# One column pair of the MLP as eight products, feature sums inside the head, modulation moved between layers

## The chip, the cores and the metric

The kernel runs on one core of a Trainium2 chip. The metric is device time in microseconds (us) of one execution; the time before is the median of 3 runs. One more execution was recorded by the hardware profiler, and all rows below come from it. The engines are named as in the profile: PE (matmul), PEld (weight load, beside PE), DVE (vector), ACT (scalar activations), POOL (GpSimd), SP (the queue that issues the loads).

## The reference

Two layers of a hybrid backbone are computed for 640 tokens: 512 sample tokens on a grid and 128 context tokens, model width 1024. Cut to what matters here, each layer is

```python
shift1, scale1, gate1, shift2, scale2, gate2 = silu(cond) @ w_mod + b_mod   # 6 x 1024
h = rms_norm(x, norm1_g) * (1 + scale1) + shift1
z = h @ w_in                      # pooling, q, k, v, LRU, gates
...
h_seq, h_final = rg_lru(conv_centred(u_lru), ...)     # scans over the tokens
merged = g0 * (pool_o @ w_branch[0]) + g1 * (attn_o @ w_branch[1]) + g2 * (lru_o @ w_branch[2])
x = x + gate1 * (merged @ w_out)
h2 = rms_norm(x, norm2_g) * (1 + scale2) + shift2
x = x + gate2 * (square(relu(h2 @ w_up)) @ w_down)    # w_up 1024 x 4096
```

All arrays are float32. The second layer's modulation (the first line) needs only the conditioning vectors, so the kernel may compute it at any time before its use.

## The kernel before, in words

**Tokens and precision.** Activations lie transposed: 128 features on the partitions, 640 tokens in two halves of 320 (`HALF`). Every operand is split into a high and a low part, and one product is three matmuls per 128 rows of weights (high x high, high x low, low x high; `product`, lines 248 to 259). So one column block of 128 output features for one half takes 8 x 3 = 24 matmuls of 128x320 in the mixers and in the first four column blocks of the MLP, and 12 where the depth is 512. Weights come by DMA into three `raw` buffers and are split by ACT (high part, line 227) and DVE (low part, line 228).

**The list of work.** `build_layer` appends items in the order in which PE is to work; the loop at the end of `hybrid_step_kernel` walks the list and issues loads and splits ahead. After each product `tick` runs one step of two queues of generators (`side_a`, `side_b`) and closures that were deferred by a number of ticks. A scheduler then orders the instructions of each engine; every engine works in that order.

**The MLP.** The 4096 columns of `w_up` are 8 blocks `b` of 512, each two pairs `e` of 256 columns. Block 0 is the **head**: a group of four items, each with 2 x 24 matmuls. It starts while the second half of `h2` is not yet made: `head` first does the first 12 matmuls of each item on the first half (`head_low`), calls `second()` (`norm_second`: statistics matmul `nps`, line 446, then DVE, ACT and POOL), and then the rest. The head's products are read out of PSUM by `evict_up` (DVE line 1190, ACT lines 1191 and 1192, DVE line 1193). The other 14 pairs are items of kind `st`: `st_body` computes a pair of column blocks over both halves by **seven** products of 12 matmuls (lines 295 to 297) in place of eight, from sums of weight blocks (POOL, lines 272 to 275, in `st_begin`) and sums of feature blocks (`T1` to `T4`). These feature sums are made once per layer by the generator `sums` (POOL lines 1236, 1239, 1246, 1256; DVE 1237, 1240, 1242, 1257, 1259; split by ACT 1227 and DVE 1228), in two parts `c` of 640 columns each and then `T4`. It is put on `side_b` when the head is over, runs a step per tick of the down products, and what is left is run (`drain`) ahead of the first `st` item:

```python
        down(0, 0, 2)
        up(1, 0)
        down(0, 4)
        up(1, 1)
        down(0, 6)
        for b in range(2, 8):
            up(b, 0)
            down(b - 1, 0, 2)
            up(b, 1)
            down(b - 1, 4, 6)
```

`down(b, m)` multiplies block `b`'s 512 squared features by two column blocks of `w_down` (four products of 12 matmuls), and DVE adds them to `x` (`x_update`, line 498).

**Modulation.** 12 chunks of 512 outputs per layer; a chunk is four items of kind `modv` (256 rows of `w_mod`), each of them four DVE instructions of 128x512 (lines 517 and 519), with a summing matmul (`mps`, line 525) and transposes (`mcol`, line 506) on PE per chunk. `mod_next()` puts the next such item behind the item just added. In layer 0's MLP, items of 6 chunks of the second layer are put behind every `up` and `down` until they are used up; the other 6 chunks are spread in the second layer's mixers. The first layer has 8 chunks in its own mixers, at the same places of the code.

**LRU.** The generator `lru` on `side_b` makes, for each of four channel blocks, the convolution, its split `xs` (ACT line 953, DVE 954), then after `LY` ticks the gate matmuls `lps` (line 964), activations, scans and the product with the gelu branch; `split_act` splits the result into `lh` for the third branch's products (`mm<-lh`).

Of the kernel before, what the change touches and what calls it, by code (L numbers as in the profile page):

```python
# [36 lines left out]
PY = 2  # L37
LY = 1
SY = 0
# [17 lines left out]
def hybrid_step_kernel(  # L57
# [285 lines left out]
    def head(its, done, evict, second=None):  # L343

        h = state["h"]
        for e, it in enumerate(its):
            head_low(it["i"])
            if e == 1 and second:
                second()
        for e, it in enumerate(its):  # L350
            evict(e, 0, product(it, 0, 0, h, 8, range(4, 8), it["ps"]))
            tick()
        for e, it in enumerate(its):
            evict(e, 1, product(it, 0, 1, h, 8))
            tick()
            done()
# [694 lines left out]
    def build_layer(l):  # L1051
# [130 lines left out]
        if l + 1 < DEPTH:  # L1182
            mod_todo.extend((l + 1, n, kk) for n in range(6) for kk in range(4))

# [10 lines left out]
        def up_body(b, e):  # L1195
# [13 lines left out]
            def body(it):  # L1209
                if (b, e) == (1, 0):  # L1210
                    drain(side_b)
# [4 lines left out]
                if (b, e) == (7, 1):  # L1216
                    del L["T"]
            return body

        def sums():  # L1220
# [13 lines left out]
            for c in range(2):  # L1234
# [14 lines left out]
                yield  # L1249
            state["h"] = None  # L1250
            out["T4"] = unit("T4", [128, 2, 4, HALF])
            b12 = None
            for c in range(2):
# [60 lines left out]
        def up(b, e):  # L1314
            add("st", up_pair(b, e), up_body(b, e), more_bias if (l, b, e) == (0, 2, 0) else
                late_h if (l, b, e) == (1, 2, 0) else None)
            items[-1]["i"] = len(items) - 1
            mod_next()

        def down(b, *ms):  # L1320
            for m in ms:
                add("k4", down_src(b, m), down_body(b, m))
                mod_next()

        def up_head(its, done):
            head(its, done, lambda *a: evict_up(0, *a), lambda: norm_second(l, 1))
            side_b.append(("sums", sums()))

        add_group("k8", [up_src(i) for i in range(4)], up_head, pre_up)
        down(0, 0, 2)  # L1330
        up(1, 0)
        down(0, 4)
        up(1, 1)
        down(0, 6)
        for b in range(2, 8):
# [4 lines left out]
        if l + 1 < DEPTH:  # L1340
            add_group("k4", [down_src(7, m) for m in range(0, 8, 2)], down_tail)
            mod_todo.extend((l + 1, n, kk) for n in range(6, 12) for kk in range(4))
        else:
# [237 lines left out]
```

## Time and profile before

| what | value |
|---|---|
| median of 3 runs | 2170.62 us (2170.19 to 2172.32) |
| the profiled execution | 2169.2 us, its span 2167.4 us |
| mean granted clock of PE | 0.99 of full speed |
| PE busy | 2104.7 us, 97% of the span |
| DVE, ACT, POOL busy | 70%, 47%, 25% of the span |
| HBM | 204.76 MB read, 101 GB/s over the span |

The span is the time from the first to the last instruction; the execution's own time is 1.8 us longer. PE's matmuls overlap: the 311 ns of a row is the length of one, not the distance between two, so PE's pace is read from counts of matmuls per stretch.

### The profile page before, as it was taken

Reading aid. Unit: us, or ns where it says so; the run is one execution under the profiler, and the core shown is the slowest. Engines: PE = TensorE matmul, PEld = TensorE weight load, DVE = VectorE, ACT = ScalarE, POOL = GpSimd, SP = SyncE. Lnnn points to the kernel's source line nnn. Section 1 sums busy time; section 2 is a strip of 40 time slices with the busy share of each in tenths; the row PEclk is TensorE's granted clock in tenths of the full one; section 3 lists DMA queues with packets and bytes.
Section 4 is the critical chain, followed back from the end, with each engine's and each line's share of the span. In section 5 each row is a group of like instructions: output and inputs, shape, how many; then the busy total and the mean of one; then the engine's idle time right before and its main releaser. Section 6 shows DMA issues by size and latency. Waiting matters only on the chain.

```text
span 2167.4 us, 35837 instructions
## 1 busy us (share of the span) xinstructions
PE 2104.7 (97%) x13892; PEld 1989.1 (92%) x13892; DVE 1507.1 (70%) x2937; ACT 1019.3 (47%) x2068; POOL 542.1 (25%) x575
## 2 busy tenths in 40 slices
PE   8999999999998899999999999999999989999999
PEld 3988899999998889899999888999999979999999
DVE  4777766667768988876677775675854777666665
ACT  4765427673244433333356654277633544333332
POOL 2444301242204221231024441012421232111110
PEclk9999999999999999999999999999999999999999
DMA  9322243324532344432341122432243212222222
GB/s 323 102 62 81 77 138 99 96 81 151 175 98 68 98 121 133 126 98 79 98 136 50 56 68 75 146 104 77 79 126 124 72 49 79 78 79 78 80 87 78
DMA packets 246914, 218.16 MB, mean 101 GB/s; under 512 B 11077, under 2 KB 214361, under 8 KB 246745
## 3 DMA queue, kind: packets, MB, share of 16 engines
q1 hardware_dynamic: 246744, 215.88, 32.7%
q8 instruction: 109, 1.79, 0.3%
q14 instruction: 61, 0.49, 0.1%
HBM read 204.76 MB, written 13.12 MB: 101 GB/s over the span
## 4 chain that ended last, share of the span: by engine, by line
PE 75%; DVE 12%; DMA 4%; ACT 4%; POOL 3%; issue 2%; SPq 0%; POOLq 0%; ACTq 0%; DVEq 0%
PE mm L256 18%; PE mm L258 17%; PE mm L257 17%; PE mm L295 3%; PE mm L297 3%; PE mm L296 3%; DVE macc L519 2%; PE o L772 2%; DVE wlo L228 1%; DMA raw<-in_w_mod_dram 1%; DVE t L465 1%; PE mmz L295 1%; PE mmz L297 1%; PE mmz L296 1%; PE ptt L759 1%
## 5 line engine op out<-in xcount | busy, mean ns | idle before, releaser
L256 PE MATMUL mm<-h,whi 128*128 128x320 f32 x1536 | 486.9, 317 | 6.0 <-DVE rl L1190 2.9
L257 PE MATMUL mm<-h,whi 128*128 128x320 f32 x1536 | 478.3, 311 | 3.2 <-DVE h L479 2.4
L258 PE MATMUL mm<-h,wlo 128*128 128x320 f32 x1536 | 477.3, 311 | 0.0
L228 DVE TENSOR_TENSOR wlo<-raw,whi 128x512 fp32r<-128x512 f32 x388 | 276.4, 721 | 115.5 <-ACT whi L227 113.5
L227 ACT ACTIVATE whi<-raw 128x512 fp32r<-128x512 f32 x388 | 239.1, 627 | 236.7 <-PE mm L257 104.7
L256 PE MATMUL mm<-u,whi 128*128 128x320 f32 x992 | 309.5, 312 | 11.3 <-ACT u L1192 7.0
L256 PEld LDWEIGHTS mm<-h,whi 128*128 128x128 f32 x1536 | 291.1, 190 | 21.5 <-issue 8.6
L257 PE MATMUL mm<-u,whi 128*128 128x320 f32 x992 | 308.1, 311 | 0.0
L258 PE MATMUL mm<-u,wlo 128*128 128x320 f32 x992 | 307.8, 310 | 0.0
L257 PEld LDWEIGHTS mm<-h,whi 128*128 128x128 f32 x1536 | 291.2, 190 | 6.0 <-DVE h L479 3.9
L258 PEld LDWEIGHTS mm<-h,wlo 128*128 128x128 f32 x1536 | 291.0, 189 | 0.1
L498 DVE SCALAR_TENSOR_TENSOR x<-mm,mod,x 128x320 f32<-128x320 f32 (+2 forms) x432 | 174.8, 433 | 107.8 <-PE mm L258 107.6
L519 DVE SCALAR_TENSOR_TENSOR macc<-raw,silc,macc 128x512 f32<-128x512 f32 x280 | 226.1, 827 | 31.2 <-DMA raw<-in_w_mod_dram 29.6
L256 PEld LDWEIGHTS mm<-u,whi 128*128 128x128 f32 x992 | 187.6, 189 | 14.5 <-ACT u L1192 7.3
L257 PEld LDWEIGHTS mm<-u,whi 128*128 128x128 f32 x992 | 187.5, 189 | 0.3 <-DVE u L1193 0.2
L258 PEld LDWEIGHTS mm<-u,wlo 128*128 128x128 f32 x992 | 187.5, 189 | 0.0
L272 POOL TENSOR_TENSOR S<-raw 128x512 f32<-128x512 f32 x28 | 38.4, 1371 | 545.5 <-DMA raw<-in_w_up_dram 424.2
L288 ACT ACTIVATE whi<-S 128x512 fp32r<-128x512 f32 x112 | 70.8, 632 | 192.4 <-PE mm L257 94.2
L289 DVE TENSOR_TENSOR wlo<-S,whi 128x512 fp32r<-128x512 f32 x112 | 87.2, 781 | 53.7 <-ACT whi L288 52.2
L295 PE MATMUL mm<-T,whi 128*128 128x320 f32 x336 | 106.4, 317 | 11.6 <-ACT rl L309 7.0
L288 ACT ACTIVATE whi<-raw 128x512 fp32r<-128x512 f32 x84 | 52.9, 630 | 125.5 <-PE mm L257 74.5
L297 PE MATMUL mm<-T,wlo 128*128 128x320 f32 x336 | 105.6, 314 | 5.1 <-DVE wlo L289 4.9
(303 smaller groups left out, 4769.7 us busy)
## 6 DMA issues: line engine op xcount, KB each, us to landing
raw<-in_w_in_dram SPq DMA_DIRECT2D x96, 512.0 KB, 4.0
raw<-in_w_mod_dram SPq DMA_DIRECT2D x80, 512.0 KB, 4.0
raw<-in_w_up_dram SPq DMA_DIRECT2D x64, 512.0 KB, 3.7
raw<-in_w_down_dram SPq DMA_DIRECT2D x64, 512.0 KB, 3.5
raw<-in_w_branch_dram SPq DMA_DIRECT2D x24, 512.0 KB, 3.5
wm<-in_w_mod_dram SPq DMA_DIRECT2D x8, 1024.0 KB, 12.3
raw<-in_w_out_dram SPq DMA_DIRECT2D x16, 512.0 KB, 4.3
xs_d<-x SPq DMA_DIRECT2D x4, 1280.0 KB, 7.8
```

Source lines behind the costliest of these rows:

```text
L227: A.activation(hi, rs, AF.Copy)
L228: V.tensor_tensor(lo, rs, f32(hi), op=OP.subtract)
L256: T.matmul(ps, wh, xh, start=(k == 0), stop=False)
L257: T.matmul(ps, wh, xl, start=False, stop=False)
L258: T.matmul(ps, wl, xh, start=False, stop=(k == nk - 1))
L288: A.activation(hi, a, AF.Copy)
L289: V.tensor_tensor(lo, a, f32(hi), op=OP.subtract)
L295: T.matmul(ps, hi[:, k, :], x[:, 0, k, :], start=start and k == 0, stop=False, skip_group_check=True)
L296: T.matmul(ps, hi[:, k, :], x[:, 1, k, :], start=False, stop=False, skip_group_check=True)
L297: T.matmul(ps, lo[:, k, :], x[:, 0, k, :], start=False, stop=k == 3, skip_group_check=True)
L498: V.scalar_tensor_tensor(xa, ps[:, a:b], mod[l][:, gate + m, j:j + 1], xa, op0=OP.mult, op1=OP.add)
L519: V.scalar_tensor_tensor(acc[j], w, silc[:, k, j:j + 1], acc[j], op0=OP.mult, op1=OP.add)
```

## The change

- `up(1, 0)`, the first `st` item of each layer, is replaced by two items of kind `k8` with `plain_body`: eight products' worth of matmuls (2 column blocks x 2 halves x 24), read out by `evict_up`. They stand directly behind the head, ahead of the down products of block 0. `up(1, 1)` is the first `st` item now.
- `sums` is put on `side_b` inside the head, right behind `norm_second`; it waits with `T4` until the plain pair has read `h` (`"h free"`). In `head`, `second()` is called one item later (`e == 2`).
- 4 in place of 6 chunks of the second layer's modulation are made in layer 0's MLP, at 2 items per block (3 in blocks 2 and 3); the other 8 in the second layer's mixers.
- `LY` is 2 in place of 1.

```diff
@@ -35,7 +35,7 @@
 AQ = 4
 AH = 4
 PY = 2
-LY = 1
+LY = 2
 SY = 0
 ORD = (4, 0, 1, 2, 3, 5, 6, 7)
 PM = ((2, 3, 6, 7), (2, 3, 6, 7))
@@ -345,7 +345,7 @@
         h = state["h"]
         for e, it in enumerate(its):
             head_low(it["i"])
-            if e == 1 and second:
+            if e == 2 and second:
                 second()
         for e, it in enumerate(its):
             evict(e, 0, product(it, 0, 0, h, 8, range(4, 8), it["ps"]))
@@ -1180,7 +1180,7 @@
         assert not mod_todo
         add_group("k8", [w_out[l][:, m * 128:m * 128 + 128] for m in range(4, 8)], out_tail)
         if l + 1 < DEPTH:
-            mod_todo.extend((l + 1, n, kk) for n in range(6) for kk in range(4))
+            mod_todo.extend((l + 1, n, kk) for n in range(4) for kk in range(4))
 
         def evict_up(b, i, half, ps):
             if i == 0 and half == 0:
@@ -1207,7 +1207,7 @@
                 defer(1, lambda: V.tensor_tensor(o[:, 1], t, f32(o[:, 0]), op=OP.subtract))
 
             def body(it):
-                if (b, e) == (1, 0):
+                if "T" not in L:
                     drain(side_b)
                 nx = it["i"] + 2
                 while nx < len(items) and items[nx - 1]["kind"] == "modv":
@@ -1215,6 +1215,15 @@
                 st_body(it, L["T"], evict, lambda: splits(nx))
                 if (b, e) == (7, 1):
                     del L["T"]
+            return body
+
+        def plain_body(b, i):
+            def body(it):
+                for half in range(2):
+                    evict_up(b, i, half, product(it, 0, half, state["h"], 8))
+                    tick()
+                if i == 1:
+                    L["h free"] = True
             return body
 
         def sums():
@@ -1247,9 +1256,10 @@
                 yield
                 put("T2", c, f2)
                 yield
-            state["h"] = None
+            while "h free" not in L:
+                yield
+            b12 = state["h"] = None
             out["T4"] = unit("T4", [128, 2, 4, HALF])
-            b12 = None
             for c in range(2):
                 f4 = two("f4")
                 t2 = out["T2"]
@@ -1315,23 +1325,26 @@
             add("st", up_pair(b, e), up_body(b, e), more_bias if (l, b, e) == (0, 2, 0) else
                 late_h if (l, b, e) == (1, 2, 0) else None)
             items[-1]["i"] = len(items) - 1
-            mod_next()
+            if (b, e) in ((2, 0), (3, 0)):
+                mod_next()
 
         def down(b, *ms):
             for m in ms:
                 add("k4", down_src(b, m), down_body(b, m))
-                mod_next()
-
-        def up_head(its, done):
-            head(its, done, lambda *a: evict_up(0, *a), lambda: norm_second(l, 1))
+                if m % 4 == 0:
+                    mod_next()
+
+        def second():
+            norm_second(l, 1)
             side_b.append(("sums", sums()))
 
-        add_group("k8", [up_src(i) for i in range(4)], up_head, pre_up)
+        add_group("k8", [up_src(i) for i in range(4)],
+                  lambda its, done: head(its, done, lambda *a: evict_up(0, *a), second), pre_up)
+        for i in range(2):
+            add("k8", up_src(4 + i), plain_body(1, i))
         down(0, 0, 2)
-        up(1, 0)
-        down(0, 4)
         up(1, 1)
-        down(0, 6)
+        down(0, 4, 6)
         for b in range(2, 8):
             up(b, 0)
             down(b - 1, 0, 2)
@@ -1339,7 +1352,7 @@
             down(b - 1, 4, 6)
         if l + 1 < DEPTH:
             add_group("k4", [down_src(7, m) for m in range(0, 8, 2)], down_tail)
-            mod_todo.extend((l + 1, n, kk) for n in range(6, 12) for kk in range(4))
+            mod_todo.extend((l + 1, n, kk) for n in range(4, 12) for kk in range(4))
         else:
             for m in range(0, 8, 2):
                 add("k4", down_src(7, m), last_body(m))
```

**The order that the scheduler makes of it, three places.** POOL in layer 0's MLP, from the first part of the sums (`f`, names behind it are tile numbers) to the weight sums `S` of the first two `st` items. Before:

```order
190 L1246 TENSOR_TENSOR f_7468<-f_7466,f_7467 128x640
191 L272 TENSOR_TENSOR S_7536<-raw 128x512
192 L273 TENSOR_TENSOR S_7537<-S_7536,raw 128x512
193 L274 TENSOR_TENSOR S_7538<-raw 128x512
194 L275 TENSOR_TENSOR S_7539<-raw,S_7537 128x512
195 L1236 TENSOR_TENSOR f_7582<-h_6964 128x640
196 L1239 TENSOR_TENSOR f_7584<-f_7582,h_6962 128x640
197 L1246 TENSOR_TENSOR f_7585<-f_7583,f_7584 128x640
198 L1256 TENSOR_TENSOR f_7638<-h_6963,T_7464 128x640
199 L1256 TENSOR_TENSOR f_7644<-h_6963,T_7464 128x640
```

and with the change:

```order
191 L1255 TENSOR_TENSOR f_7261<-f_7259,f_7260 128x640
192 L1245 TENSOR_TENSOR f_7398<-h_6964 128x640
193 L1248 TENSOR_TENSOR f_7400<-f_7398,h_6962 128x640
194 L1255 TENSOR_TENSOR f_7401<-f_7399,f_7400 128x640
195 L1266 TENSOR_TENSOR f_7642<-h_6963,T_7257 128x640
196 L1266 TENSOR_TENSOR f_7677<-h_6963,T_7257 128x640
197 L272 TENSOR_TENSOR S_7710<-raw 128x512
198 L273 TENSOR_TENSOR S_7711<-S_7710,raw 128x512
199 L274 TENSOR_TENSOR S_7712<-raw 128x512
200 L275 TENSOR_TENSOR S_7713<-raw,S_7711 128x512
```

The four weight sums of the first `st` item stood between the two parts of the feature sums; now all feature sums stand ahead of them.

DVE in layer 0's MLP, from the third readout of the item `up(2, 0)` on (`macc` are the modulation's accumulators). Before:

```order
916 L313 TENSOR_TENSOR rl<-mmz,rl 128x320
917 L519 SCALAR_TENSOR_TENSOR macc<-raw,silc,macc 128x512
918 L1205 SCALAR_TENSOR_TENSOR rl<-rl 128x320
919 L1202 TENSOR_SCALAR rl<-mm 128x320
920 L228 TENSOR_TENSOR wlo<-raw,whi 128x512
921 L1207 TENSOR_TENSOR u_8210<-rl,u_8210 128x320
922 L228 TENSOR_TENSOR wlo<-raw,whi 128x512
923 L1207 TENSOR_TENSOR u_8209<-rl,u_8209 128x320
924 L498 SCALAR_TENSOR_TENSOR x_6486<-mm,mod_132,x_6486 128x320
925 L519 SCALAR_TENSOR_TENSOR macc<-raw,silc,macc 128x512
926 L498 SCALAR_TENSOR_TENSOR x_6486<-mm,mod_132,x_6486 128x320
927 L519 SCALAR_TENSOR_TENSOR macc<-raw,silc,macc 128x512 x2
```

and with the change:

```order
891 L313 TENSOR_TENSOR rl<-mmz,rl 128x320
892 L228 TENSOR_TENSOR wlo<-raw,whi 128x512
893 L1205 SCALAR_TENSOR_TENSOR rl<-rl 128x320
894 L1202 TENSOR_SCALAR rl<-mm 128x320
895 L228 TENSOR_TENSOR wlo<-raw,whi 128x512
896 L1207 TENSOR_TENSOR u_8163<-rl,u_8163 128x320
897 L1207 TENSOR_TENSOR u_8162<-rl,u_8162 128x320
898 L498 SCALAR_TENSOR_TENSOR x_6486<-mm,mod_132,x_6486 128x320 x2
```

Four accumulations stood among the readouts of this stretch; now none does, and the next ones follow further on.

ACT in layer 0's mixers, at the split `xs` of the LRU's second channel block and the first activation of its `lps` (`lu`, `g`: readouts of other products on PE, one for each half). Before:

```order
382 L912 ACTIVATE lu<-mm 128x192
383 L913 ACTIVATE lu<-mm 128x128
384 L953 ACTIVATE xs<-xc 128x644
385 L909 ACTIVATE lu<-mm 128x320
386 L965 ACTIVATE lt_3912<-lps,vecT_126 128x322 x2
```

and with the change:

```order
381 L953 ACTIVATE xs<-xc 128x644
382 L909 ACTIVATE lu<-mm 128x320
383 L227 ACTIVATE whi<-raw 128x512 x2
384 L912 ACTIVATE lu<-mm 128x192
385 L913 ACTIVATE lu<-mm 128x128
386 L1014 ACTIVATE g<-mm 128x320
387 L965 ACTIVATE lt_3912<-lps,vecT_126 128x322 x2
```

Between the split and the gate matmuls, PE now has the products behind two more readouts.

## Rows read from the trace of the kernel before

**Rows 1.** The page, busy time of each engine (share of the span, instructions).
```profile
PE 2104.7 (97%) x13892; PEld 1989.1 (92%) x13892; DVE 1507.1 (70%) x2937; ACT 1019.3 (47%) x2068; POOL 542.1 (25%) x575
```
**Rows 2.** Busy time by stretch; the first line names the columns.
```profile
core 0: us, PE busy (x) PEld busy (x) DVE busy (x) ACT busy (x) POOL busy (x), PEclk, DMA share, GB/s
386.00:400.00 14.00, 11.59 (x58) 10.98 (x58) 5.76 (x8) 8.21 (x16) 0.00 (x0) 0.76 0.44 133
500.00:640.00 140.00, 138.48 (x925) 132.66 (x924) 92.30 (x165) 46.90 (x94) 21.00 (x18) 1.00 0.49 147
586.00:596.00 10.00, 8.48 (x57) 8.00 (x56) 10.00 (x17) 2.56 (x5) 2.57 (x2) 1.00 0.53 155
645.00:688.00 43.00, 38.46 (x249) 37.79 (x248) 40.62 (x74) 24.31 (x55) 13.72 (x11) 0.96 0.25 74
688.00:714.00 26.00, 16.38 (x92) 15.89 (x91) 19.77 (x29) 8.43 (x15) 10.72 (x7) 0.87 0.06 21
714.00:950.00 236.00, 225.66 (x1491) 214.23 (x1490) 207.44 (x381) 85.31 (x165) 54.73 (x36) 1.00 0.41 123
1460.00:1475.00 15.00, 12.57 (x75) 12.08 (x74) 7.82 (x14) 9.89 (x19) 0.00 (x0) 0.89 0.47 138
1560.00:1700.00 140.00, 139.93 (x946) 137.09 (x946) 74.70 (x132) 47.71 (x90) 25.32 (x23) 1.00 0.39 120
1715.00:1750.00 35.00, 31.72 (x200) 30.46 (x199) 32.78 (x57) 21.04 (x48) 13.58 (x10) 0.95 0.20 61
1750.00:1782.00 32.00, 22.76 (x128) 21.74 (x127) 21.66 (x33) 10.38 (x18) 10.39 (x7) 0.84 0.06 17
1782.00:2100.00 318.00, 318.00 (x2171) 317.94 (x2169) 215.55 (x417) 121.02 (x235) 69.08 (x52) 1.00 0.27 83
```
**Rows 3.** PE in order of time: start, length, instruction, [idle before and its releaser].
```profile
650.64 0.54 PE L446 MATMUL nps<-acc,ones 128*128 128x320 f32 x1 [2.21 <-DVE acc L410]
...
664.19 0.61 PE L256 MATMUL mm<-h,whi 128*128 128x320 f32 x1 [2.33 <-DVE rl L1190]
...
694.80 0.61 PE L256 MATMUL mm<-u,whi 128*128 128x320 f32 x1 [4.28 <-DVE x L498]
...
708.89 0.64 PE L295 MATMUL mm<-T,whi 128*128 128x320 f32 x1 [5.33 <-ACT rl L309]
...
1758.66 0.64 PE L256 MATMUL mm<-u,whi 128*128 128x320 f32 x1 [7.05 <-ACT u L1192]
```
**Rows 4.** POOL in order of time, layer 0's MLP.
```profile
683.80 1.96 POOL L272 TENSOR_TENSOR S<-raw 128x512 f32<-128x512 f32 x1 [10.93 <-DMA raw<-in_w_up_dram]
...
690.07 1.53 POOL L1236 TENSOR_TENSOR f<-h 128x640 f32<-128x640 f32 x1
```
**Rows 5.** DVE in order of time, layer 0's MLP.
```profile
693.24 0.82 DVE L1242 TENSOR_TENSOR f<-f,h 128x640 f32<-128x640 f32 x1 [6.33 <-POOL f L1239]
```
**Rows 6.** Whom PE waited for, 714 to 950 us: total, times, longest.
```profile
PE mm L295 <- DVE rl L313: 4.6, 5, 1.4
PE mm L297 <- DVE wlo L289: 4.0, 4, 1.2
PE mmz L297 <- DVE wlo L289: 1.2, 2, 0.7
```
**Rows 7.** DVE by line, 714 to 950 us: busy us, mean ns of one | idle before.
```profile
L519 DVE SCALAR_TENSOR_TENSOR macc<-raw,silc,macc 128x512 f32<-128x512 f32 x76 | 62.3, 836 | 6.3 <-DMA raw<-in_w_mod_dram 6.1
```
**Rows 8.** DVE by line and form, 645 to 714 us.
```profile
L1228 DVE TENSOR_TENSOR T<-f,T 128x640 fp32r<-128x640 f32 x8 | 8.7, 1084 | 0.0
...
L1190 DVE TENSOR_SCALAR rl<-mm 128x320 f32<-128x320 f32 x8 | 3.7, 477 | 0.0
```
**Rows 9.** PE at the LRU's second channel block, layer 0, in order of time.
```profile
391.10 0.64 PE L964 MATMUL lps<-xs,bs 128*128 128x322 f32 x1 [2.18 <-ACT xs L953]
...
509.36 0.41 PE L256 MATMUL mm<-lh,whi 128*128 128x320 f32 x1
```
**Rows 10.** DVE in order of time, split of the LRU's result, layer 0.
```profile
490.15 2.89 DVE L845 TENSOR_TENSOR lh<-lru,lh 128x1280 fp32r<-128x1280 f32 x2 [0.54 <-ACT lh L844]
```

## The prediction

> **What bounds the kernel now.** The page's busy times come first: PE is busy for 97% of the span [rows 1], so only two things can change the time much: how many matmuls there are, and the stretches in which PE does not run at its pace. The second view, busy time by stretch, gives that pace. From 1782 to 2100 us PE does 2171 matmuls in 318 us without a gap, 0.1465 us each [rows 2]. What a stretch loses is its length less its count times 0.1465:
>
> - 688 to 714 us (layer 0, ahead of and in the first `st` item): 26 - 92 x 0.1465 = 12.5 us lost; 1750 to 1782 us (the same place in layer 1): 32 - 128 x 0.1465 = 13.2 us.
> - 714 to 950 us (layer 0's MLP with the modulation): 236 - 1491 x 0.1465 = 17.6 us.
> - 386 to 400 and 1460 to 1475 us (the LRU's second channel block): 14 - 58 x 0.1465 = 5.5 us and 15 - 75 x 0.1465 = 4.0 us.
> - 645 to 688 and 1715 to 1750 us (the head and the norm in it): 43 - 249 x 0.1465 = 6.5 us and 35 - 200 x 0.1465 = 5.7 us.
> - 586 to 596 us (start of the output projection, layer 0): 1.65 us.
>
> The third view, PE in order of time, says what ended the waits [rows 3]. A wait costs more than its length: the granted clock is 0.87 and 0.84 of full in the two sum stretches and 0.76 at the LRU [rows 2], that is, PE runs for some matmuls at 1.2 in place of 2.4 GHz behind a wait. In layer 0 the two waits of 4.28 and 5.33 us make 12.5 us, a factor of 1.3.
>
> Why PE waits at 694.80 and 708.89 us is read on POOL and DVE. POOL stood for 10.93 us, until 683.80 us, for the DMA of the first `st` item's weights, and then did its four weight sums; the second part of the feature sums, queued behind them, started at 690.07 us [rows 4]. DVE, in order, waited 6.33 us for POOL's sum [rows 5], and behind that stood the additions to `x` that free PSUM (PE's first wait), then the last sums that ACT had to split ahead of its PSUM copies (PE's second). Layer 1 has one such wait of 7.05 us and smaller ones.
>
> **The change, part by part.**
>
> *Eight products for seven.* A plain pair is 2 x 2 x 24 = 96 matmuls where an `st` item has 7 x 12 = 84: 24 more over both layers, on PE's path: **+3.5 us**. DVE, ACT and POOL get less: four weight sums on POOL and three weight splits less per layer.
>
> *Feature sums in the head.* The order shows them ahead of the weight sums, so POOL's wait for a DMA no longer holds them. Is there room? By 688 us DVE had done 7 of a layer's 18 sum instructions (before too they began behind the norm), and it was busy for 40.6 of 43 us [rows 2], so I take it that it does no more in the head. PE then has 96 plain and 96 down matmuls, 28.1 us, to the first `st` item, and 72 more, 10.5 us, until that item's last product needs `T4`: 38.6 us. DVE's work in them: 11 sums at 0.82 [rows 5] to 1.08 us [rows 8] = 9.0 to 11.9 us; four readouts, each a maximum and a split of 0.48 [rows 8] = 3.8; eight additions to `x` and eleven weight splits, bounded by 0.48 and 1.08 each [rows 8], taken at 0.65 = 12.4; one modulation item in layer 0, 4 x 0.84 [rows 7] = 3.3. About 30 us of 38.6: it fits, so the waits of both stretches go, 12.5 + 13.2 us. POOL and DVE still meet there, and I leave 1 us per layer standing: **-23.7 us**. The bounds are 0 us left, and 9 us per layer left (the lock, below).
>
> *Statistics one item later.* PE waited 2.21 us at 650.64 us for DVE's last square sum [rows 3]. 11 more matmuls, 1.6 us, now cover most of that. But the next wait, 2.33 us at 664.19 us for DVE's readout, is set by the chain from these statistics through the norm, which starts no earlier; it grows by the same 1.6 us. **0 us**; bounds -1 (no modulation instruction in that chain of layer 0 any more) to +1 (a longer wait, a lower clock behind it).
>
> *A third less modulation in layer 0's MLP.* There DVE is busy for 207.4 of 236 us, 88%, of which 62.3 us are accumulations [rows 2, 7]; in layer 1's MLP, which has none, it is 215.6 of 318 us, 68%, and PE never waits [rows 2]. PE's waits, 9.8 us [rows 6], are all for DVE. The rest of the 17.6 us is the steps behind the waits and the chunks' own matmuls, which move and are not saved. Now a block of about 53 us (2 x 84 + 4 x 48 matmuls) holds two items, 6.7 us of DVE: 68 + 13 = 81%, in blocks 2 and 3 three: 87%. I take 9 of some 11 us as saved, 2 left: **-9 us**; bounds -11 and 0.
>
> *The eight items in layer 1's mixers.* They land from about 1560 us on, where DVE is busy for 74.7 of 140 us. 8 x 3.3 = 27 us make it 101, still 73%. Layer 0 has them at the same places of the code: 92.3 of 140 us, and it loses 1.65 us at 586 to 596 us, where DVE is busy throughout, while layer 1 loses nothing [rows 2]. **+1.65 us**; bounds 0 and +4. Loads move along; SP's queue and the DMA engines are busy for 0.49 there in layer 0, without a wait of PE for a DMA.
>
> *`LY` = 2.* PE reached the gate matmuls 2.18 us too early [rows 9]. The order shows two more products of 24 matmuls, 7.0 us, between the split and the gate matmuls: the wait and the slow matmuls behind it go, in both layers: **-9.5 us**. Each channel block ends one tick later, four in all, 12 to 24 matmuls each: 7 to 14 us. The result's split was done at 493.04 us [rows 10] and first needed at 509.36 us [rows 9], so 16.3 us of room cover it.
>
> **The sum:** 3.5 - 23.7 + 0 - 9 + 1.65 - 9.5 = -37.1 us. The profiled execution took 2169.2 us, its span 2167.4; it lies 1.4 us under the median of 2170.6. So 2132.1 us against its time, **2133.5 us** against the median.
>
> **The rivals.**
>
> *DVE and POOL lock each other.* The three-operand splits of the sums took 1.08 us on average where a like instruction alone took 0.82 [rows 5, 8], so some ran beside POOL and were held. POOL's part in the 38.6 us is six feature sums and four weight sums at 1.5 to 2.0 us [rows 4], about 17 us. If DVE stood for all of it, 30 + 17 = 47 us against 38.6: 8.4 us of waits per layer, with the factor 1.3 some 11. I price half a case, 9 us per layer in place of 1: 2133.5 + 16 = 2149.5 us. Against it: the measured excess is 0.26 us per instruction, not a whole POOL instruction. The Trainium skill, page "SBUF — State Buffer", section "Who interferes with whom", says that a vector instruction with two SBUF inputs and a GpSimd instruction that reads SBUF exclude each other, and the second "fully blocks"; that speaks for the full 11 us per layer, 2153.5 us, and the mean of rows 8 for less.
>
> *Density is not what makes PE wait in layer 0's MLP.* If the waits came from the position of single accumulations, all 11 us stay: 2133.5 + 9 = 2142.5 us. For it: blocks 2 and 3 still stand at 87%, the share of now. Against it: no waits without modulation.
>
> *The LRU's wait moves to its end.* If the four ticks push the split behind its use, what `LY` gains is given back: 2143 us. 16.3 us of room speak against it.
>
> *All goes, and the slow matmuls in the head too.* 2133.5 - 2 - 2 - 1.65 - 3 = about 2125 us.
>
> *Slower.* In the head, sums and readouts share DVE, in order. Were each of the six sum instructions that wait for POOL to stand as long as the one at 693.24 us, 6.33 us [rows 5], DVE would stand for 38 us per layer, about 29 beyond its room of 38.6 - 30; times 1.3 that is 38 us per layer, 76 in all, in place of the 2 left: 2133.5 + 74 = 2207 us. It decides from the point at which these waits pass 20 us per layer. Against it: that wait came from POOL's DMA, which now stands behind the sums.
>
> *The change does not do what it says:* some other instruction holds the sums as before, and the waits merely move; with 3.5 us more of matmuls and the LRU unchanged, about 2168 us. The order shows otherwise.
>
> **How the numbers follow.** Chances: forecast (2127 to 2139) 0.57; all goes 0.09; modulation waits stay 0.12; LRU 0.07; lock 0.10; slower 0.02; nothing happens 0.03. A measurement of this kernel tells about 0.2%, 4.3 us, from no change. Faster by more: 0.57 + 0.09 + 0.12 + 0.07 + 0.10 = 0.95; the same 0.03; slower 0.02. The range from 2123 to 2144 takes in the first four cases, 0.85, and leaves out the lock, the slower case and no change.
>
> **What would show it.** In the changed profile, the stretch from the head to the end of the first `st` item should have no wait of PE over 2 us but the one for DVE's readout at the head's middle, which should be near 3.5 us; POOL's first weight sum should come behind all feature sums; layer 0's MLP should lose under 8 us behind that in place of 17.6, with DVE near 80%; no wait at the gate matmuls; in layer 1's mixers, waits of some 1.5 us at the output projection. PE's matmuls should be 24 more. A wait of PE for `lh`, a DVE that stands for POOL in the plain pair, or a count of matmuls per stretch under the pace there would prove the sum wrong.

## The result and the profile after

| | before | changed |
|---|---|---|
| median | 2170.40 us | 2135.83 us (2134.76 to 2140.25, 4 runs) |
| ratio to before, 95% interval | | 0.9844 [0.9827, 0.9861] |
| span of the profiled execution | 2167.4 us | 2133.0 us |

The changed kernel is 1.6% faster; 2133.5 us was forecast, with a range of 2123 to 2144. The span fell by 34.4 us. Of the page, the busy times of the engines (share of the span, instructions); against [rows 1] there are 24 matmuls more, and PE is busy for a larger share of a shorter span:

```profile
PE 2095.2 (98%) x13916; PEld 1985.1 (93%) x13916; DVE 1487.4 (70%) x2925; ACT 1009.3 (47%) x2058; POOL 524.5 (25%) x567
```

Busy time by stretch, the same places as [rows 2] at their new times; the first line names the columns:

```profile
core 0: us, PE busy (x) PEld busy (x) DVE busy (x) ACT busy (x) POOL busy (x), PEclk, DMA share, GB/s
382.00:396.00 14.00, 12.49 (x86) 12.23 (x85) 12.73 (x19) 5.62 (x13) 0.00 (x0) 1.00 0.51 150
582.00:592.00 10.00, 8.77 (x58) 8.28 (x57) 9.77 (x17) 2.57 (x5) 2.59 (x2) 1.00 0.56 157
640.00:690.00 50.00, 45.83 (x291) 45.17 (x290) 48.67 (x77) 28.88 (x64) 20.95 (x14) 0.93 0.16 46
690.00:714.00 24.00, 22.46 (x150) 21.70 (x149) 19.92 (x39) 10.84 (x21) 6.12 (x4) 1.00 0.34 98
714.00:930.00 216.00, 216.00 (x1467) 213.42 (x1466) 164.55 (x319) 80.20 (x155) 42.31 (x32) 1.00 0.35 105
1425.00:1440.00 15.00, 13.47 (x92) 13.21 (x91) 13.39 (x21) 5.63 (x13) 1.09 (x5) 1.00 0.54 161
1526.00:1685.00 159.00, 157.56 (x1053) 151.48 (x1053) 110.92 (x191) 61.77 (x117) 30.82 (x28) 1.00 0.44 133
1685.00:1725.00 40.00, 35.80 (x223) 35.15 (x222) 38.67 (x65) 24.97 (x55) 16.27 (x12) 0.91 0.19 54
1725.00:1760.00 35.00, 31.88 (x217) 31.45 (x216) 27.88 (x43) 14.73 (x28) 10.89 (x6) 1.00 0.16 46
1760.00:2070.00 310.00, 310.00 (x2116) 309.94 (x2116) 202.83 (x404) 114.75 (x221) 61.96 (x48) 1.00 0.27 82
```

The last row gives the same pace as before, 310 / 2116 = 0.1465 us per matmul; the second, layer 0's output projection, loses 1.5 us for 1.65 before. What each other row loses is read as in the prediction, length less count times 0.1465:

| place | before | after | difference | forecast |
|---|---|---|---|---|
| 24 more matmuls | | | +3.5 | +3.5 |
| sums, layer 0 and layer 1 | 12.5 + 13.2 | 2.0 + 3.2 | -20.5 | -23.7 |
| heads, layer 0 and layer 1 | 6.5 + 5.7 | 7.4 + 7.3 | +2.5 | 0 |
| layer 0's MLP with modulation | 17.6 | 1.1 | -16.5 | -9 |
| layer 1's mixers from the third branch on | 1.4 | 4.7 | +3.3 | +1.65 |
| LRU's second block, both layers | 5.5 + 4.0 | 1.4 + 1.5 | -6.6 | -9.5 |
| **sum** | | | **-34.3** | **-37.1** |

The sum of the rows is the difference of the spans to 0.1 us. The stretches outside the list cancel: behind the LRU's second block of layer 0 (396 to 496 us) 1.0 us less is lost than before, and from 930 to 1080 us, where the rest of layer 0's modulation now stands, 1.5 us more. Where the waits of [rows 3] and [rows 9] stood, PE in order of time now shows these (start, length, instruction, [idle before and its releaser]):

```profile
387.53 0.41 PE L258 MATMUL mm<-h,wlo 128*128 128x320 f32 x1 [1.51 <-DVE wlo L228]
...
645.97 0.81 PE L446 MATMUL nps<-acc,ones 128*128 128x320 f32 x2 [0.60 <-DVE acc L410]
...
659.15 0.60 PE L256 MATMUL mm<-h,whi 128*128 128x320 f32 x1 [3.58 <-DVE rl L1190]
...
696.22 0.42 PE L256 MATMUL mm<-u,whi 128*128 128x320 f32 x1 [0.75 <-DVE rl L1190]
...
710.13 0.41 PE L297 MATMUL mm<-T,wlo 128*128 128x320 f32 x1 [0.53 <-DVE wlo L289]
...
1703.73 0.61 PE L256 MATMUL mm<-h,whi 128*128 128x320 f32 x1 [3.60 <-DVE rl L1190]
...
1745.08 0.38 PE L256 MATMUL mm<-u,whi 128*128 128x320 f32 x1 [3.12 <-DVE x L498]
```

Where layer 0's sums made PE wait 4.28 and 5.33 us, at the first down product and in the first seven-product item, it now waits 0.75 and 0.53 us; the 7.05 us of layer 1 are 3.12 us. POOL in order of time, layer 0, shows the cause turned round against [rows 4]: the last feature sums, then the wait for the weights, then the weight sums, so that nothing but they wait for that DMA.

```profile
680.38 4.29 POOL L1266 TENSOR_TENSOR f<-h,T 128x640 f32<-128x640 f32 x2
697.93 1.29 POOL L272 TENSOR_TENSOR S<-raw 128x512 f32<-128x512 f32 x1 [13.26 <-DMA raw<-in_w_up_dram]
```

### The profile page after: what moved, and what is told of

Same layout as the page of the kernel before. It is cut to its first block, busy times and chain, and to the rows that moved or that the text cites. A ratio compares the mean times of both kernels' runs of the same rounds, so it can differ in the third digit from the quotient of the medians.

```text
span 2133.0 us, 35830 instructions
## 1 busy us (share of the span) xinstructions
PE 2095.2 (98%) x13916; PEld 1985.1 (93%) x13916; DVE 1487.4 (70%) x2925; ACT 1009.3 (47%) x2058; POOL 524.5 (25%) x567
## 4 chain that ended last, share of the span: by engine, by line
PE 80%; DVE 10%; ACT 4%; DMA 3%; issue 1%; POOL 1%; SPq 0%; ACTq 0%; DVEq 0%; POOLq 0%
PE mm L256 19%; PE mm L257 18%; PE mm L258 18%; PE mm L295 4%; PE mm L297 4%; PE mm L296 4%; PE o L772 2%; DVE wlo L228 2%; PE mmz L296 1%; PE mmz L297 1%; PE mmz L295 1%; DVE t L465 1%; DVE macc L519 1%; PE ptt L759 1%; PE mps L1438 1%
## 5 line engine op out<-in xcount | busy, mean ns | idle before, releaser
L256 PE MATMUL mm<-h,whi 128*128 128x320 f32 x1600 | 507.3, 317 | 10.3 <-DVE rl L1190 7.2
L258 PE MATMUL mm<-h,wlo 128*128 128x320 f32 x1600 | 498.1, 311 | 3.1 <-DVE wlo L228 3.0
L257 PE MATMUL mm<-h,whi 128*128 128x320 f32 x1600 | 498.3, 311 | 2.7 <-DVE h L479 2.0
L228 DVE TENSOR_TENSOR wlo<-raw,whi 128x512 fp32r<-128x512 f32 x396 | 287.4, 735 | 112.6 <-ACT whi L227 110.7
L256 PEld LDWEIGHTS mm<-h,whi 128*128 128x128 f32 x1600 | 303.5, 190 | 25.6 <-ACT h L478 7.6
L257 PEld LDWEIGHTS mm<-h,whi 128*128 128x128 f32 x1600 | 303.6, 190 | 5.4 <-DVE h L479 2.9
L258 PEld LDWEIGHTS mm<-h,wlo 128*128 128x128 f32 x1600 | 303.4, 190 | 4.2 <-DVE wlo L228 4.1
L519 DVE SCALAR_TENSOR_TENSOR macc<-raw,silc,macc 128x512 f32<-128x512 f32 x280 | 217.5, 799 | 36.8 <-DMA raw<-in_w_mod_dram 35.1
L272 POOL TENSOR_TENSOR S<-raw 128x512 f32<-128x512 f32 x26 | 34.3, 1320 | 531.8 <-DMA raw<-in_w_up_dram 319.6
L288 ACT ACTIVATE whi<-S 128x512 fp32r<-128x512 f32 x104 | 65.8, 633 | 198.6 <-PE mm L257 144.0
L289 DVE TENSOR_TENSOR wlo<-S,whi 128x512 fp32r<-128x512 f32 x104 | 73.0, 703 | 44.4 <-ACT whi L288 44.1
L297 PE MATMUL mm<-T,wlo 128*128 128x320 f32 x312 | 96.5, 309 | 0.5 <-DVE wlo L289 0.5
L295 PE MATMUL mm<-T,whi 128*128 128x320 f32 x312 | 96.4, 309 | 0.0
```

The source lines that it names most:

```text
L228: V.tensor_tensor(lo, rs, f32(hi), op=OP.subtract)
L256: T.matmul(ps, wh, xh, start=(k == 0), stop=False)
L257: T.matmul(ps, wh, xl, start=False, stop=False)
L258: T.matmul(ps, wl, xh, start=False, stop=(k == nk - 1))
L288: A.activation(hi, a, AF.Copy)
L289: V.tensor_tensor(lo, a, f32(hi), op=OP.subtract)
```

## Experiments: each part alone

Where an expectation below lists rival accounts, they are called the first, second and third in their order. Each ratio is to the kernel before, run beside the changed one; its median lies between 2166.9 and 2170.8 us from group to group, so runs of different groups are compared by their ratios.

**`LY` = 2 alone**, on the kernel before.

```diff
-LY = 1
+LY = 2
```

> The kernel before with LY = 2 alone. In the changed kernel's trace the two LRU stretches (386 to 500 and 1460 to 1560 us before) lose 3.9 us where before lost 11.7 us. If LY makes that by itself: 7.8 us faster, about 2162.6 us, no wait at the gate matmuls and a wait of about 1.5 us for a weight split (DVE, line 228) at the same place. The prediction's term: 9.5 us faster, 2160.9. Rival, the wait moves to the LRU's end (a wait of PE for lh): 2168 to 2171 us.

Measured: 2162.03 us beside 2169.50, ratio 0.9968 [0.9957, 0.9979]; 7.5 us by the medians, 6.9 by the ratio, as the first account has it (7.8 us). PE no longer waits at the gate matmuls. Whom PE waited for from 380 to 400 us (total, times, longest), the only line:

```profile
PE mm L258 <- DVE wlo L228: 1.5, 1, 1.5
```

The wait was not only removed, a smaller one took its place. DVE in order of time in the changed kernel, where the same 1.51 us stands at 387.53 us: the weight split (line 228) comes behind the split of the attention's result, 2.88 us for two instructions, and accumulations of the modulation.

```profile
382.01 2.88 DVE L845 TENSOR_TENSOR ah<-attn,ah 128x1280 fp32r<-128x1280 f32 x2
...
386.79 0.69 DVE L228 TENSOR_TENSOR wlo<-raw,whi 128x512 fp32r<-128x512 f32 x1
```

**The modulation alone**, on the kernel before: `range(4)` for `range(6)`, and the spacing of the change in `up` and `down`.

```diff
-            mod_next()
+            if (b, e) in ((2, 0), (3, 0)):
+                mod_next()
...
-                mod_next()
+                if m % 4 == 0:
+                    mod_next()
```

> The kernel before with the modulation as in the change (4 chunks at 2 or 3 items per block in layer 0's MLP, 8 in layer 1's mixers), nothing else. If DVE's density makes PE's waits: the 15 us that the waits cost in layer 0's MLP go, about 3 us come in layer 1's mixers: 12 us faster, about 2158.3 us. The prediction's terms (-9 + 1.65): 2163.0 us. Rival, the position of single accumulations makes them: not faster, 2170 to 2172 us.

Measured: 2156.60 us, ratio 0.9947 [0.9934, 0.9959], 11.5 us by the ratio and 12.9 by the medians. One wait of 1.5 us is left, from 714 to 930 us, of the 9.8 us there before. The first account holds, and the prediction's terms were too small.

**The plain pair, the sums in the head and the later statistics alone**: the changed kernel with `LY` = 1 and the old modulation.

> The changed kernel with LY = 1 and the modulation as before: the plain pair, the sums in the head and the statistics one item later alone. If the three parts add up: +3.5 us of matmuls, -20.6 in the two stretches of the sums, +2.3 in the heads: 14.8 us faster, about 2155.6 us. The prediction's terms (+3.5 - 23.7): 2150.2 us. Rival, the parts lean on each other (with dense modulation DVE has no room for the sums): 2160 us or more, with waits of PE in layer 0 and not in layer 1.

Measured: 2155.35 us, ratio 0.9940 [0.9928, 0.9953]; 13.0 us by the ratio, 14.2 by the medians. The three parts alone make 7.5 + 12.9 + 14.2 = 34.6 us by their medians; the whole change makes that too. By the ratios the parts make 31.4 us and the whole 33.9. They add up, and none leans on another by more than the measurement can tell.

## Experiments: what the sums needed

**Sums queued behind the head**, as before; the plain pair stays.

```diff
         def second():
             norm_second(l, 1)
+
+        def up_head(its, done):
+            head(its, done, lambda *a: evict_up(0, *a), second)
             side_b.append(("sums", sums()))
 
-        add_group("k8", [up_src(i) for i in range(4)],
-                  lambda its, done: head(its, done, lambda *a: evict_up(0, *a), second), pre_up)
+        add_group("k8", [up_src(i) for i in range(4)], up_head, pre_up)
```

> The changed kernel with the sums queued behind the head, as before; the plain pair stays. If the plain pair does it (weights of the first seven-product item come two items later, so POOL does the feature sums first, and there is more matmul time): within 3 us of the changed kernel, 2134 to 2139 us. If being queued in the head does it: the sums end several us later, DVE has to do them among the additions to x, and 5 to 10 us per layer come back: 2146 to 2156 us.

Measured: 2145.63 us, ratio 0.9906 [0.9889, 0.9924], that is 13 us worse than the changed kernel by the ratios and 7 by the spans of the profiled executions (2140.0 against 2133.0). The plain pair by itself does not do it. POOL in order of time:

```profile
689.69 1.78 POOL L272 TENSOR_TENSOR S<-raw 128x512 f32<-128x512 f32 x1 [12.35 <-DVE T L1237]
691.55 1.42 POOL L273 TENSOR_TENSOR S<-S,raw 128x512 f32<-128x512 f32 x1
692.93 1.88 POOL L274 TENSOR_TENSOR S<-raw 128x512 f32<-128x512 f32 x1
694.77 1.76 POOL L275 TENSOR_TENSOR S<-raw,S 128x512 f32<-128x512 f32 x1
696.49 2.00 POOL L1255 TENSOR_TENSOR f<-f,f 128x640 f32<-128x640 f32 x1
698.57 3.61 POOL L1266 TENSOR_TENSOR f<-h,T 128x640 f32<-128x640 f32 x2
```

The weight sums stand ahead of the last feature sums again, and those end at 702.2 us, some 17 us later than in the changed kernel (684.7 us). PE waits 5.3 us in layer 0 and 4.4 us in layer 1 for an addition to `x`.

**No plain pair**: `up(1, 0)` is a seven-product item again, in its old place; the sums stay in the head, without their wait for the plain pair's reading of `h`.

```diff
-            while "h free" not in L:
-                yield
...
-        for i in range(2):
-            add("k8", up_src(4 + i), plain_body(1, i))
         down(0, 0, 2)
+        up(1, 0)
+        down(0, 4)
         up(1, 1)
-        down(0, 4, 6)
+        down(0, 6)
```

> The changed kernel without the plain pair: its pair of columns is a seven-product item again at the place of before; sums queued in the head. 24 matmuls less, 3.5 us. If the order on POOL (feature sums ahead of the weight sums) is what mattered: about 2132 us. If the matmul time ahead of the first seven-product item mattered: DVE has about 30 us of work for 24.5 us of matmuls, 5.4 us short per layer, times 1.3: -3.5 + 14 = 2146 us. If the order turns back as well: 2153 us.

Measured: 2146.21 us, ratio 0.9907 [0.9891, 0.9922]: about the 2146 us of the second account, although 24 matmuls less are done (the kernel before took 2166.87 us beside it; by the ratios it is 14 us worse than the changed kernel, by the spans 11.5). Whom PE waited for in layer 0, 640 to 715 us, the two longest of four lines:

```profile
PE mm L256 <- DVE rl L1190: 6.8, 1, 6.8
PE mm L257 <- DVE u L1193: 3.7, 1, 3.7
```

These two have different causes. The 6.8 us stand in the middle of the head, where the changed kernel waits 3.58 us. Without the plain pair a modulation item comes earlier in the list, and DVE stands for its load in the chain that makes the norm. PE, then DVE in order of time:

```profile
661.74 0.61 PE L256 MATMUL mm<-h,whi 128*128 128x320 f32 x1 [6.85 <-DVE rl L1190]
...
649.02 0.88 DVE L517 TENSOR_SCALAR macc<-raw,silc 128x512 f32<-128x512 f32 x2 [2.58 <-DMA raw<-in_w_mod_dram]
...
650.48 0.48 DVE L437 SCALAR_TENSOR_TENSOR nw<-nps,nw 128x320 f32<-128x320 f32 x1
```

So some 3 us of this run's loss come from where the modulation lands, not from DVE's room for the sums. The 3.7 us behind the head, for its last readout, are what missing cover costs: there, with no plain pair ahead of the down products, DVE's sums and splits hold up that readout. From behind the midpoint wait through the first seven-product item, layer 0 (668 to 715 us) loses 7.3 us, where the changed kernel (665.4 to 714 us) loses 2.0. In layer 1, which has no modulation in its MLP, 6.8 us (1719 to 1790 us) stand against 3.2 (1708.5 to 1780 us). So the gain takes both: the place in the head makes the order on POOL, and the plain pair buys DVE the matmul time in which to do the work. Its price, 3.5 us, is less than these 8.9 us; in layer 1 alone it gains about 2 us.

## Experiments: what made the modulation's waits

**4 chunks at the old spacing**, behind every item until they are used up.

> The changed kernel with its 4 chunks in layer 0's MLP put behind every item until they are used up, the spacing of before. If density on DVE makes the waits: two thirds of the 15 us come back, about 2146 us, with waits of PE for DVE as before in the first blocks. If the count of chunks matters: 2136 us.

Measured: 2149.98 us, ratio 0.9925 [0.9909, 0.9940], some 17.5 us worse than the changed kernel by the ratios, 15 by the spans. Of that 3.7 us are lost from 690 to 720 us, beside the sums, and 10.8 us from there to 930 us. Giving back the whole modulation part would cost 12.9 us by its medians above, so the smaller count by itself saves nothing. Whom PE waited for, 715 to 1040 us, the first of four lines:

```profile
PE mm L295 <- DVE rl L313: 5.4, 4, 2.4
```

**6 chunks, evenly spaced**, one item behind every down product.

> The changed kernel with 6 chunks in layer 0's MLP, one item behind every down product (4 per block, evenly), 6 in layer 1's mixers. By the prediction's account DVE would be busy for some 93% there, as much as before or more: if that share makes the waits, 10 to 15 us come back less some 1 us in layer 1's mixers, 2145 to 2150 us. If the waits come from accumulations right at the seven-product items' readouts, which have none here: 2135 to 2138 us.

Measured: 2146.09 us, ratio 0.9907 [0.9891, 0.9923], some 14 us worse by the ratios, 11.5 by the spans. No item is put behind a seven-product item here, and PE waits all the same, now for a weight split, once per block (715 to 1040 us):

```profile
PE mm L297 <- DVE wlo L289: 7.6, 5, 2.4
```

DVE by line, 714 to 1040 us (busy, mean ns | idle before), shows that DVE's busy time is not the whole of it: the loads of the modulation come late too, and DVE, in order, stands 20 us for them.

```profile
L519 DVE SCALAR_TENSOR_TENSOR macc<-raw,silc,macc 128x512 f32<-128x512 f32 x76 | 55.8, 746 | 20.1 <-DMA raw<-in_w_mod_dram 19.9
```

**Same count and density as the change, other position**: each item behind the second down product of a pair, next to the seven-product item.

```diff
-                if m % 4 == 0:
+                if m % 4 == 2:
                     mod_next()
```

> The changed kernel with the same 4 chunks at the same 2 or 3 items per block, each item behind the second down product of a pair (next to the following seven-product item) in place of the first. Count and density are those of the changed kernel; only the position differs. If DVE's share decides whether PE waits: no waits in layer 0's MLP, within 2 us of the changed kernel, 2134 to 2138 us. If the position decides (accumulations, and DVE's wait for their load, right before the splits that the seven-product item needs): waits of 1 to 2.4 us for a weight split (line 289) once or twice per block, as in the run with 4 items per block: 6 to 11 us slower, 2142 to 2147 us.

Measured: 2138.27 us, ratio 0.9853 [0.9836, 0.9869], the same as the changed kernel within the intervals, with no wait of PE from 715 to 1040 us. So of these two positions neither makes PE wait, and density does: two or three items per block of some 53 us make no wait at either, four or more do. DVE alone in one stretch of 53 us, busy time (instructions), clock, DMA share, GB/s; of the changed kernel:

```profile
767.00:820.00 53.00, 42.52 (x81) 1.00 0.37 110
```

of the kernel with 4 chunks at the old spacing:

```profile
767.00:820.00 53.00, 46.86 (x86) 1.00 0.42 130
```

and of 6 chunks evenly:

```profile
767.00:820.00 53.00, 42.87 (x83) 1.00 0.37 115
```

80% is free of waits in the first, and 81% is not in the last, which has DVE standing for loads besides. A limit in DVE's share can't be read from these; one in items per block can. Whether DVE's work or its late loads make the waits of the last was not separated.

## Experiments: the head and layer 1's wait

**Statistics at `e == 1`** again.

> The changed kernel with the second statistics at e == 1, as before. In the changed kernel PE waits 0.6 us for the statistics and 3.6 us for the readout behind them. If the chain from DVE's last square sum through the norm sets the end of the two waits, only their split changes: waits of 2.2 and 2 us, the time within 1.5 us of the changed kernel, 2134.5 to 2137. If one item later really covers PE's wait: 1.6 us per layer more, 2139. If it is what made the heads 0.8 and 1.4 us longer: 2133.6.

Measured: 2136.79 us, ratio 0.9853 [0.9840, 0.9867]; PE waits 2.2 and 2.0 us as the first account has it, but also 1.4 us each for a later readout and an addition to `x` in layer 0. The changed kernel has 0.9844 above and 0.9836 [0.9822, 0.9849] below. The difference of 2 to 4 us is not clear of the intervals: whether one item later is worth anything stays open.

**The first two POOL sums on DVE**, in both layers.

```diff
-                G.tensor_tensor(f12, part(b12, 0, c), part(b12, 1, c), op=OP.add)
+                E = V if c == 0 else G
+                E.tensor_tensor(f12, part(b12, 0, c), part(b12, 1, c), op=OP.add)
...
-                G.tensor_tensor(f1, f12, part(b11, 0, c), op=OP.subtract)
+                E.tensor_tensor(f1, f12, part(b11, 0, c), op=OP.subtract)
```

> The changed kernel with the two POOL sums of the first part (f12 and f1 of c = 0) on DVE, in both layers, so that POOL does no sum beside the norm in the head. If POOL's sums hold DVE's steps of the norm (1.16 us each for 0.65, and a split of 1.82 for 0.48): the readout comes some 2 us earlier, PE's wait of 3.6 us shrinks to 1.5 or 2, 3 to 5 us faster over both layers. If DVE has no room for two more sums, 1.6 us per layer: waits for readouts or additions to x grow by as much, 3 us slower. If both: within 1.5 us.

Measured: 2139.18 us, ratio 0.9840 [0.9824, 0.9855]: no gain. The mechanism is there. DVE in order of time, the norm's split just ahead of the readout, of the changed kernel:

```profile
656.79 1.82 DVE L479 TENSOR_TENSOR h<-t,h 128x320 fp32r<-128x320 f32 x1
```

and of this kernel:

```profile
656.97 0.48 DVE L479 TENSOR_TENSOR h<-t,h 128x320 fp32r<-128x320 f32 x1
```

PE's wait for the readout fell from 3.58 to 0.96 us in layer 0, and to 0.95 us in layer 1. But the time came back further on: 1.0 us in either head for the norm's own splits, in layer 0 3.1 us for a weight split and 1.6 for a readout (0.75 in the changed kernel), in layer 1 1.3 us for a readout, and the 3.1 us for an addition to `x` stay too. POOL's first weight sum in layer 0 still waits for its load, until 699.58 us (697.93 in the changed kernel). This is the third account, both at once: with the head shorter, what follows is late.

**The changed kernel again, and with a later load in layer 1.** In layer 0, where a modulation load is issued ahead of them, the weights of the first seven-product item keep POOL waiting until 697.93 us, 38.8 us behind the head's readout wait; in layer 1, without them, POOL starts at 1738.86 us, 35.1 us behind it, while DVE is still at its last sums. The edit ties that load to the plain pair's third readout.

```diff
                 r = raw_p.tile([128, 1024], F32, tag="raw", name="raw")
+                if "hold" in it:
+                    G.tensor_copy(r[:, 0:4], it["hold"]())
...
         up(1, 1)
+        if l == 1:
+            [it for it in items if it["kind"] == "st"][-1]["hold"] = lambda: f32(L["u2", 1][0][0][:, 1, 1, 0:4])
```

> The changed kernel once more, on the same chip as the two that follow, since they should differ from it by 2 to 5 us only. Ratio to the kernel before 0.984 to 0.985, the waits of PE as in its first profile: 0.6 and 3.6 us in both heads, 3.1 us for an addition to x in layer 1, about 1.5 us at the LRU's second block in both layers.

> The changed kernel with the weights of layer 1's first seven-product item loaded some 3 us later (a copy of four columns on POOL ties the load to the plain pair's third readout), as in layer 0 where modulation loads hold it up. If DVE's last sums are held by POOL's weight sums beside them (1.91 and 1.55 us on DVE for 0.82 and 0.48): these instructions are short again, PE's wait of 3.12 us in layer 1 shrinks to about 1 us, 2 to 2.5 us faster than the changed kernel. If the wait is from DVE's order alone (T4's splits ahead of the additions to x): the wait stays at 3 us, no change. If the late load is too late: PE waits for the weight split at the first seven-product item instead, 1 to 4 us slower.

Measured on one chip: the changed kernel 2136.20 us, ratio 0.9836 [0.9822, 0.9849]; with the late load 2133.39 us, 0.9826 [0.9810, 0.9841]. The medians differ by 2.8 us, where 2 to 2.5 were expected, but the intervals overlap; the profile is plainer. DVE in order of time, the last sum of `T4`, the readout behind it and the additions to `x`, of the changed kernel in its first profile, with the two weight sums on POOL that run beside them:

```profile
1741.10 1.91 DVE L1237 TENSOR_TENSOR T<-f,T 128x640 fp32r<-128x640 f32 x1
1742.92 1.55 DVE L1193 TENSOR_TENSOR u<-rl,u 128x320 fp32r<-128x320 f32 x1
1744.39 1.58 DVE L498 SCALAR_TENSOR_TENSOR x<-mm,mod,x 128x320 f32<-128x320 f32 x4
...
1740.70 1.62 POOL L273 TENSOR_TENSOR S<-S,raw 128x512 f32<-128x512 f32 x1
1742.29 1.84 POOL L274 TENSOR_TENSOR S<-raw 128x512 f32<-128x512 f32 x1
```

and with the late load, where POOL's first weight sum starts at 1744.02 us (the edit adds two lines, so line numbers are two higher):

```profile
1739.91 0.82 DVE L1239 TENSOR_TENSOR T<-f,T 128x640 fp32r<-128x640 f32 x1
1740.65 0.48 DVE L1195 TENSOR_TENSOR u<-rl,u 128x320 fp32r<-128x320 f32 x1
1741.05 1.58 DVE L500 SCALAR_TENSOR_TENSOR x<-mm,mod,x 128x320 f32<-128x320 f32 x4
```

The same instructions take 0.82 and 0.48 us with POOL idle, 1.91 and 1.55 us beside it, and PE's wait of 3.12 us shrinks to 0.3 us. Beside POOL each ends 0.3 to 0.7 us behind the POOL instruction that it met (1742.32 and 1744.13 us), so it was held for nearly all that was left of that one. That the wait is DVE held by POOL, not DVE's order, is shown; the order is the same in both.

## Why the prediction was right, and where it was off

The time was right to 2.3 us, by a sum of terms of which all but the first were off. Four came out 10.3 us worse than forecast and one 7.5 us better; that so little was left of them is luck. The mechanisms of the sums, the modulation and `LY` hold, each shown by a run; the sizes are what failed.

- **Eight products**: +3.5 us, 24 matmuls, as forecast. What they buy, DVE's room ahead of the first seven-product item, was the step the sum rested on, and the run without the pair bears it out: 8.9 us more are lost where that room is, apart from what the modulation does there. The premise that DVE "does no more in the head" was wrong on the safe side: in layer 0, 37 us behind the statistics (by 683 us), it had done 11 of the 18 sums, not 7.
- **Sums**: -20.5 for -23.7 us. The mechanism, weight sums on POOL ahead of feature sums, is shown by the run with the sums behind the head. "I leave 1 us per layer standing" was too little in layer 1, where 3.2 us are left. That is the rival of DVE and POOL holding each other, at a fraction of its price: two instructions that met POOL, instead of 9 us per layer. The Trainium skill, page "SBUF — State Buffer", section "Who interferes with whom", has a DVE instruction with two SBUF inputs contend with a GpSimd instruction that reads SBUF, by an exclusive lock; the 1.91 and 1.55 us agree. My reason against it, the mean excess of 0.26 us in [rows 8], mixed instructions that met POOL with those that did not.
- **Statistics**: the wait of 0.60 us and one of 3.58 us for the readout, forecast "near 3.5", are as said. In layer 1 the head's wait was 0.58 us before and is 3.60 now: there PE had done the matmuls ahead of it at a granted clock of 0.87 (1718.1 to 1731.4 us), so they took longer and covered more of the chain. The rows lose 2.5 us more than before, beyond the bound of +1. The chain is not the miss: up to the end of the readout's wait the two heads lose 9.2 us for 9.4 before. Behind it they lose 5.5 us for 2.7, and the clock there is lower. The 10 us from the end of that wait, before (layer 0, layer 1) and changed (columns as above):

```profile
664.00:674.00 10.00, 9.81 (x57) 9.84 (x58) 10.00 (x22) 7.03 (x17) 1.76 (x1) 0.83 0.01 2
1731.00:1741.00 10.00, 9.07 (x58) 8.57 (x59) 10.00 (x21) 6.95 (x17) 1.76 (x1) 1.00 0.00 0
...
659.00:669.00 10.00, 9.85 (x49) 9.88 (x50) 10.00 (x21) 6.55 (x15) 4.13 (x2) 0.70 0.01 2
1703.60:1713.60 10.00, 9.87 (x50) 9.90 (x51) 10.00 (x20) 6.59 (x15) 4.14 (x2) 0.71 0.00 0
```

So the bound for "a lower clock behind it" was too small, at least in this execution (last section).
- **Modulation**: -16.5 for -9 us, the largest miss. Two steps failed. The base of 68% was taken from layer 1 and each item added at full length, so blocks came to 81 and 87%; measured were 42.52 of 53 us, 80%, from 767 to 820 us, and 73 to 74% from there to 926 us. And "9 of some 11 us as saved" left out that what stood behind the waits goes with them: 17.6 us were lost, 1.1 are. The granted clock of the stretch was 1.00 before too [rows 2], so slow matmuls can be little of it; what the 7.8 us beside the waits were is open, but for the chunks' own matmuls, which moved. With the 1.5 us that now stand from 930 us on and the next term, the modulation gains 11.7 us for 7.35 forecast, as the run with it alone has it. The rival that position makes the waits fell with the run at the other position.
- **Layer 1's mixers**: +3.3 for +1.65 us, within its bounds. The waits at the output projection came as forecast, 0.79 and 0.64 us; the rest is in part the chunks' own summing matmuls and transposes, which I had let move for nothing. By PE's lines 32 of them are busy for 6.0 us from 1526 to 1685 us, 1.3 us more than as many others at the pace.
- **`LY`**: -6.6 for -9.5 us. "The wait and the slow matmuls behind it go" was right for the gate matmuls, and the step left out what is late next: a weight split on DVE, 1.5 us in each layer, shown by `LY` alone. No wait for `lh` appeared.

## What to carry to other kernels

Where an in-order helper engine has work that waits for a load, everything queued behind it waits too: put what needs no load ahead of it, and give the engine that must then do the work enough cover, even if that costs some extra matmuls. When spacing filler work, count items per period beside the helper engine's busy share, and expect nearly the whole loss of the stretch, waits and what follows them, to go or stay together. When an experiment moves a part in the list, check in its trace what else moved with it. For each wait that is removed, look for the next one within a microsecond or two on the same engine, and for POOL work that starts beside two-input DVE work.

## What was not expected of the hardware

The same wait costs different amounts in two executions of one program. In the changed kernel's two profiles PE waits 3.12 us for the same addition to `x` in layer 1. The second profile's line, beside that of 1745.08 us above:

```profile
1746.03 0.61 PE L256 MATMUL mm<-u,whi 128*128 128x320 f32 x1 [3.12 <-DVE x L498]
```

Ten us from the end of that wait, by stretch (columns as above), in the first profile:

```profile
1745.00:1755.00 10.00, 9.92 (x68) 9.95 (x69) 6.61 (x16) 2.21 (x4) 0.61 (x1) 1.00 0.18 53
```

and in the second:

```profile
1746.00:1756.00 10.00, 9.97 (x50) 10.00 (x51) 4.86 (x12) 0.85 (x2) 0.55 (x1) 0.71 0.16 53
```

With a granted clock of 1.00 PE does 68 matmuls in them, with 0.71 only 50, that is, part of them at 1.2 in place of 2.4 GHz: 18 x 0.1465 = 2.6 us. Ahead of it both profiles show the same wait at the head's middle, 3.60 us. The prediction's factor of 1.3 on a wait was taken from one stretch of one execution, and a difference of 2 or 3 us between two runs of this kernel may be no more than this. What decides it was not found.
